# Block 2 of a transformer pair: half of V from unsplit fp32 operands by token halves, and eight modulation steps moved to VectorE

## The chip, the cores and the metric

The kernel runs on one core of a Trainium2 chip. The metric is device microseconds of one execution of the whole program; less is better. Weights are read from HBM once per execution. TensorE (PE) does the matmuls, VectorE (DVE), ScalarE (ACT) and GpSimd (POOL) the rest, and SyncE (SP) issues the weight transfers.

## The reference

The reference runs two blocks on 256 tokens of width 1024, all in fp32. The first is an attention block with layer norm and a mixture of 32 experts, four for each token. The second has two layers (l = 0, 1) whose norms are modulated by a conditioning vector. Cut to what the change touches:

```python
c_act = jax.nn.silu(c)
for i in range(2):
    mod = jnp.einsum('bd,dm->bm', c_act, w_mod[i]) + b_mod[i]
    sh_a, sc_a, gt_a, sh_f, sc_f, gt_f = jnp.split(mod, 6, axis=-1)
    h = modulate(rmsnorm(x, g_mix_pre[i]), sh_a, sc_a)        # h*(1+scale)+shift
    qkv = jnp.einsum('bsd,de->bse', h, w_qkv[i])
    o = attention(q, k, v)                 # stick-breaking for i=0, forgetting for i=1
    x = x + gt_a[:, None, :] * rmsnorm(o @ w_o[i], g_mix_post[i])
    h = modulate(rmsnorm(x, g_ffn_pre[i]), sh_f, sc_f)
    gate = causal_depthwise_conv(h @ w_ffn_gate[i], w_conv[i], b_conv[i])
    y = (jax.nn.silu(gate) * (h @ w_ffn_up[i])) @ w_ffn_down[i]
    x = x + gt_f[:, None, :] * rmsnorm(y, g_ffn_post[i])
```

## The kernel before, in words

Tokens stand in two halves of 128 (t = 0, 1). All weights come through one DMA queue of SP in the order of a list that is written out in `make_stream` and `stream_l2`. Its items are units of 128 x 2048 fp32, 1 MB each. Two units that follow each other share a slot of 2 MB. There are five slots `wu_m`, one `wu_x` and three `wu_y`; the last two kinds are open from the first attention or the first norm until the later experts. A transfer is issued when `take`, which hands units to the program in the order of the list, has moved past both units of an older slot. So what is loaded ahead is limited by slots, and a pair counts as one slot whatever stands in it.

In block 2 nearly every product is made of split operands. `split` turns a unit into a high part wH (a cast on ACT) and a rest wL (a subtraction on DVE), two pieces each; the activations have hH and hL likewise. `mm3` then runs three fp32r matmuls, high by high, low by high and high by low (lines 161 to 163). An FFN unit of gate or up is 48 such matmuls of 256 columns. `pre` makes the normed and modulated h: xs on DVE, transposes on PE, hF from scale and shift (ACT and DVE), then hH and hL. In the gate/up loop of `ffn`, unit n is multiplied while unit n+1 is split; behind that split stands the work on the unit before: for a gate unit the convolution on DVE and silu on ACT, for an up unit the product cv with the gate on DVE, its cast aH on ACT and its rest aL on DVE. Each engine runs its instructions in order.

The modulation vectors, six of 1024 for each layer, come in groups (l, g) of two vectors, and each group takes eight steps, one unit of w_mod each. A step on PE (`mod_step`, line 264) is four fp32 matmuls on strips of 32 columns. On DVE (`mod_dve`, lines 316 and 318) a step is two operations over 1024 columns into `macc`; `mod_sum` then adds the partitions with four matmuls, and `flush_mod` transposes the result into place. Before, groups (0, 1) and (1, 0) are DVE's, in the attention loop and in the down stage of layer 0; the rest are PE's: `fill` puts them where PE has little to do, in numbers set by `MOD_A`, `MOD_PRE` and `MOD_MID`. A group that is interrupted leaves its partial sum in `mpart`, and DVE adds it at the end. `warm` issues bf16 matmuls whose result nobody reads. The MoE ends in `norm2`, the second layer norm; V is the first product of each layer, two units for each half of its columns, followed in layer 1 by the forget gate (`strips`, line 580).

The core of the stream's bookkeeping, in which a freed pair lets the next transfer go:

```python
            if i % 2 == 0:
                self.pools[self.where[i - 2]][1] += 1
                self.pump()
```

Of the kernel before, what the change touches and what calls it, by code (L numbers as in the profile page):

```python
# [18 lines left out]
P = 128  # L19
# [42 lines left out]
class Stream:  # L62


    def __init__(self, nc, srcs):
        self.nc = nc
        self.srcs = srcs
        self.pools = {}
        self.order = []
        self.tiles = {}  # L70
        self.where = {}
        self.issued = 0
        self.taken = 0
# [19 lines left out]
    def pump(self):  # L93
        while self.issued < self.hold:
            for key in self.order:
                if self.pools[key][1] > 0 and self.issued < self.limit.get(key, 1 << 30):
                    break
            else:
                return
            i = self.issued  # L100
            self.pools[key][1] -= 1
            t = self.pools[key][0].tile([P, 2, UNIT], F32, name=f"wu_{key}", tag=f"wu_{key}")
            n = min(2, len(self.srcs) - i)
            if isinstance(self.srcs[i], Pair):
# [8 lines left out]
            self.issued += n  # L113
# [5 lines left out]
    def take(self):  # L119
        i = self.taken  # L120
        if i > 0:
            self.tiles.pop(i - 1)
            if i % 2 == 0:
                self.pools[self.where[i - 2]][1] += 1
                self.pump()
        self.taken += 1
        return self.tiles[i]

# [8 lines left out]
class Kernel:  # L137
# [45 lines left out]
    def run(self):  # L183
        tc, nc, ap = self.tc, self.nc, self.ap
        with ExitStack() as st:
# [16 lines left out]
            self.prs = keep.tile([P, 2], F32, name="prs")  # L202
            self.mhalf = keep.tile([P, 4], F32, name="mhalf")
# [13 lines left out]
    def make_stream(self):  # L217
# [12 lines left out]
        m(MOD_A)  # L230

# [35 lines left out]
    def fill(self, n, pool, pause=False, tag="acc"):  # L267
# [3 lines left out]
        for i in range(n):  # L271
# [11 lines left out]
            if end:  # L283
                sb = pool.tile([P, 512], F32, name="modsb", tag="modsb", bufs=1)

                def late(sb=sb, ps=self.mps, part=self.mpart, l=l, g=g):
                    if part is None:
                        nc.scalar.copy(sb, ps)
                    else:
                        nc.vector.tensor_tensor(sb, ps, part, op=ALU.add)  # L290
                    self.mod_tail = (sb, l, g)

                self.mps = self.mpart = None
# [5 lines left out]
    def pause_mod(self):  # L299
# [4 lines left out]
        if self.mpart is None:  # L304
            part = self.mpart = self.keep.tile([P, 512], F32, name="mpart", tag="mpart")
            return lambda: self.nc.scalar.copy(part, ps)
        part = self.mpart
        return lambda: self.nc.vector.tensor_tensor(part, ps, part, op=ALU.add)
# [11 lines left out]
    def mod_sum(self, acc, l, g, pool, part, tag="acc"):  # L320
# [7 lines left out]
        if part:  # L328
            nc.vector.tensor_tensor(sb, ps, self.mpart, op=ALU.add)
            self.mpart = None  # L330
        else:
            nc.scalar.copy(sb, ps)
# [269 lines left out]
    def norm1(self):  # L602
# [67 lines left out]
        partial = self.fill(MOD_A - 2, a2, True, "sc")  # L670
# [11 lines left out]
        self.warm(WARM[2], "sc", self.cst.bitcast(BF16))  # L682
# [229 lines left out]
    def norm2(self, banks, lnp):  # L912
        nc = self.nc
# [4 lines left out]
        for t in range(2):  # L918
            self.layer_stats(lambda h: banks[t][h], t, mv, rs)
        nm = m1.tile([P, 2], F32, name="nm2")  # L920
        for t in range(2):
            nc.vector.scalar_tensor_tensor(nm[:, t:t + 1], mv[:, t, 0:1], -1.0, rs[:, t:t + 1], op0=ALU.mult, op1=ALU.mult)
            lo, hi = slice(0, 512), slice(512, D)
            nc.scalar.activation(x[:, t, hi], banks[t][1], AF.Identity, bias=nm[:, t:t + 1], scale=rs[:, t:t + 1])
            nc.vector.scalar_tensor_tensor(x[:, t, lo], banks[t][0], mv[:, t, 0:1], lnp[:, 0, lo], op0=ALU.subtract, op1=ALU.mult)
            (nc.vector if t else nc.gpsimd).tensor_tensor(x[:, t, hi], x[:, t, hi], lnp[:, 0, hi], op=ALU.mult)
            (nc.vector if t else nc.gpsimd).tensor_tensor(x[:, t, hi], x[:, t, hi], lnp[:, 1, hi], op=ALU.add)
            nc.vector.scalar_tensor_tensor(x[:, t, lo], x[:, t, lo], rs[:, t:t + 1], lnp[:, 1, lo], op0=ALU.mult, op1=ALU.add)
# [155 lines left out]

    def spread(self, l, m, gname, a, gg=None):
# [17 lines left out]
    def post(self, t, y, gg, a2, tag, last=False):  # L1103
# [5 lines left out]
        for h in range(2):  # L1109
            nc.scalar.activation(self.junk, y[h], AF.Square, scale=1.0 / 32, accum_out=ss[:, h:h + 1])  # L1110
            if t == 1 and not last:
# [4 lines left out]
        if t == 1 and not last:  # L1116
            self.rms(self.prs[:, 0:1], self.xss[:, 0, :])
        for h in range(2):
            nc.vector.scalar_tensor_tensor(self.x[:, t, hs[h]], tmp[h], ss[:, 2:3], self.x[:, t, hs[h]], op0=ALU.mult, op1=ALU.add)
        if last:  # L1120
# [3 lines left out]
    def attention2(self, l, a, a2):  # L1124
# [5 lines left out]
        vps = [self.bank("mm") for _ in range(2)]  # L1130
# [7 lines left out]
        def first():  # L1138
            if l == 0:
                self.w_next = self.split(self.st.take(), 2)  # L1140

        if l == 0:
            self.warm(WARM[1], "tr", self.cst.bitcast(BF16))
        self.pre(l, "g_mix_pre", 0, a, a2, ("oH", "oL"), MOD_PRE[l], first, vps[0], l == 0, WARM2[l])
        cur = self.w_next
        self.token_unit(vps, self.hH, self.hL, cur, 0, (0, 1), NK)
        hH, hL = self.hH, self.hL
        nxt = self.split(self.st.take(), 2)
        for n in range(1, 4):
            cur = nxt  # L1150
            if n == 2:
                vps = [self.bank("sc") for _ in range(2)]
            self.token_unit(vps, hH, hL, cur, 4 * (n % 2), (0, 1), NK)
            nxt = self.split(self.st.take(), 2)
# [125 lines left out]
        for i in range(10):  # L1280
# [20 lines left out]
            if stick and i == 6:  # L1301
                self.mod_sum(macc, 0, 1, a2, DVE_MOD[0, 1] > 0)
# [42 lines left out]
    def ffn(self, l, a, a2):  # L1345
# [26 lines left out]
        cvs = {}  # L1372
        for n in range(NF):
# [12 lines left out]
            cur = self.split(self.st.take(), 2)  # L1386
            if pend is not None:
# [30 lines left out]
        if l == 0:  # L1418
            self.mod_sum(macc, 1, 0, a2, False, "sc")
        for t in range(2):  # L1420
# [86 lines left out]
```

## Time and profile before

| what | value |
|---|---|
| median of 3 runs | 1715.05 us (1714.19 to 1716.04) |
| the profiled execution | 1715.33 us, its span 1713.7 us |
| busy share of the span | PE 97%, DVE 43%, ACT 28%, POOL 5% |
| DMA over the span | 585 MB, 341 GB/s in the mean |
| MoE | from about 115 to 1051 us |
| layer 0 / layer 1 of block 2 | from about 1058 / 1384 us |

The time is measured by the device, the span runs from the first to the last record of the profile, so 1.6 us lie outside it. Shares of busy time are means over the whole span; a stage's limit is read from its own waits. Matmul records of PE overlap, so the time of one is read from start to start; an fp32 matmul leaves two records.

### The profile page before, as it was taken

The page shows a single profiled execution, that of the slowest core. Times are in us where ns is not written, and L with a number is a line of the kernel's source. Part 1 is how long each engine was busy: PE and PEld are TensorE (multiplying, and loading weights), DVE is VectorE, ACT ScalarE, POOL GpSimd, SP SyncE. Part 2 cuts the span into 40 slices and gives each one's busy share as a digit, 9 for nine tenths or more (in the row PEclk, how much of TensorE's full clock was granted, in tenths as well). Part 3 has the DMA queues.
Part 4 walks back from the last instruction along what each step waited for, and adds up shares of the span by engine and source line. Part 5 has one row for each costly group of instructions (what it writes and reads, how often), then busy time and mean ns, then how long its engine had stood idle before and what let it go on. Part 6 is the DMA issues. An engine that isn't in the chain of part 4 may idle for free.

```text
span 1713.7 us, 22958 instructions
## 1 busy us (share of the span) xinstructions
PE 1658.3 (97%) x9678; PEld 980.9 (57%) x9678; DVE 739.9 (43%) x1196; ACT 484.6 (28%) x806; POOL 77.8 (5%) x113
## 2 busy tenths in 40 slices
PE   9999999999999999999899997999999999999998
PEld 7973333333333333333333333886999869889996
DVE  5662121221212212121122115896666866776654
ACT  4530000000001000000010002555555365565543
POOL 0000000000000020000000001121000003100000
PEclk9999999999999999999999999999999999999999
DMA  9879999999999999999999999856855966485430
GB/s 294 323 279 427 428 428 428 428 427 428 426 427 428 428 428 427 427 427 427 426 428 428 428 427 414 345 197 235 328 196 197 373 266 221 161 333 188 181 123 25
DMA packets 59090, 584.85 MB, mean 341 GB/s; under 512 B 8816, under 2 KB 10312, under 8 KB 13544
## 3 DMA queue, kind: packets, MB, share of 16 engines
q1 hardware_dynamic: 57176, 577.95, 82.1%
q0 software_dynamic: 1808, 5.41, 1.3%
q8 instruction: 77, 1.26, 0.3%
q14 instruction: 29, 0.24, 0.0%
HBM read 582.05 MB, written 1.28 MB: 340 GB/s over the span
## 4 chain that ended last, share of the span: by engine, by line
PE 40%; DMA 6%; DVE 3%; issue 1%; ACT 1%; POOL 0%; DVEq 0%; POOLq 0%; ACTq 0%
DMA wu_m<-w_dn 6%; PE ps_mm L161 5%; PE ps_mm L163 5%; PE ps_mm L162 5%; PE ps_sc L161 3%; PE ps_sc L162 3%; PE ps_sc L163 3%; PE ps_mm L738 3%; PE ps_tr L806 2%; PE modps L264 2%; PE ps_acc L161 1%; PE ps_acc L163 1%; PE ps_acc L162 1%; DVE macc L318 1%; DVE wL L156 1%
## 5 line engine op out<-in xcount | busy, mean ns | idle before, releaser
L156 DVE TENSOR_TENSOR wL<-wu_m,wH 128x1024 fp32r<-128x1024 f32 x226 | 266.5, 1222 | 132.9 <-ACT wH L155 128.8
L738 PE MATMUL ps_mm<-wu_m,xg 128*64 128x512 f32 x1200 | 279.1, 600 | 5.5 <-DMA wu_m<-w_gu 5.1
L155 ACT CAST wH<-wu_m 128x1024 fp32r<-128x1024 f32 x226 | 225.8, 1049 | 95.0 <-PE ps_mm L162 66.1
L806 PE MATMUL ps_tr<-wu_m,aT 128*64 128x512 f32 x800 | 179.7, 595 | 19.2 <-DMA wu_m<-w_dn 19.2
L161 PE MATMUL ps_mm<-hH,wH 128*128 128x256 f32 x608 | 174.9, 288 | 0.0
L738 PEld LDWEIGHTS ps_mm<-wu_m,xg 128*64 128x64 f32 x1200 | 79.7, 137 | 165.8 <-issue 143.8
L163 PE MATMUL ps_mm<-hL,wH 128*128 128x256 f32 x608 | 172.0, 283 | 0.2 <-DVE hL L1082 0.2
L162 PE MATMUL ps_mm<-hH,wL 128*128 128x256 f32 x608 | 171.9, 283 | 0.0
L806 PEld LDWEIGHTS ps_tr<-wu_m,aT 128*64 128x64 f32 x800 | 57.0, 137 | 138.2 <-issue 101.2
L161 PEld LDWEIGHTS ps_mm<-hH,wH 128*128 128x128 f32 x608 | 116.4, 191 | 7.8 <-issue 6.5
L163 PEld LDWEIGHTS ps_mm<-hL,wH 128*128 128x128 f32 x608 | 116.5, 192 | 0.4 <-DVE hL L1082 0.4
L162 PEld LDWEIGHTS ps_mm<-hH,wL 128*128 128x128 f32 x608 | 116.5, 192 | 0.0
L810 DVE SCALAR_TENSOR_TENSOR yL<-ps_tr,gs,yH 128x512 fp32r<-128x512 f32 x32 | 24.0, 751 | 204.9 <-ACT yH L809 204.9
L718 ACT COPY gs<-ps_tr 128x512 f32<-128x512 f32 x32 | 18.8, 586 | 330.1 <-PE ps_tr L715 330.1
L792 DVE COPY gs<-ps_tr 128x1 f32<-128x1 f32 x32 | 5.1, 159 | 235.7 <-ACT s L790 235.7
L738 PE MATMUL ps_mm<-wu_y,xg 128*64 128x512 f32 x448 | 103.5, 598 | 1.1 <-DMA wu_y<-w_gu 1.1
L162 PE MATMUL ps_sc<-hH,wL 128*128 128x256 f32 x352 | 99.7, 283 | 0.0
L161 PE MATMUL ps_sc<-hH,wH 128*128 128x256 f32 x352 | 99.6, 283 | 0.0
L163 PE MATMUL ps_sc<-hL,wH 128*128 128x256 f32 x352 | 99.6, 283 | 0.0
L738 PE MATMUL ps_mm<-wu_x,xg 128*64 128x512 f32 x400 | 91.2, 598 | 0.0
L809 ACT ACTIVATE yH<-ps_tr,gs 128x512 fp32r<-128x512 f32 x32 | 22.0, 687 | 233.3 <-PE ps_tr L806 233.3
L753 ACT ACTIVATE sg<-g 128x512 f32<-128x512 f32 x32 | 20.2, 630 | 212.4 <-DVE g L752 212.4
(344 smaller groups left out, 2472.7 us busy)
## 6 DMA issues: line engine op xcount, KB each, us to landing
wu_m<-w_gu SPq DMA_DIRECT2D x75, 2048.0 KB, 25.6
wu_m<-w_dn SPq DMA_DIRECT2D x48, 2048.0 KB, 26.1
wu_y<-w_gu SPq DMA_DIRECT2D x28, 2048.0 KB, 35.7
wu_x<-w_gu SPq DMA_DIRECT2D x25, 2048.0 KB, 24.6
wu_m<-w_mod SPq DMA_DIRECT2D x48, 1024.0 KB, 7.1
wu_m<-w_fg_u SPq DMA_DIRECT2D x44, 1024.0 KB, 8.5
wu_y<-w_dn SPq DMA_DIRECT2D x14, 2048.0 KB, 38.1
wu_m<-w_qk SPq DMA_DIRECT2D x24, 1024.0 KB, 8.8
```

What stands on the lines that cost most here:

```text
L155: nc.scalar.copy(h[:, sl], src[:, sl])
L156: nc.vector.tensor_tensor(lo[:, sl], src[:, sl], h[:, sl].bitcast(F32), op=ALU.subtract)
L161: mm(out, lh, rh, start=start, stop=False)
L162: mm(out, ll, rh, start=False, stop=False)
L163: mm(out, lh, rl, start=False, stop=stop)
L264: self.nc.tensor.matmul(ps[32 * j:32 * j + 32, :], self.cact[:, k:k + 1].to_broadcast([P, 32]), u[:, 512 * j:512 * j + 512], start=start, ...
L718: nc.scalar.copy(gs, g)
L738: mm(ab[i][64 * h:64 * h + 64, :], self.chunk(xg, k), u[:, c:c + 512], start=False, stop=k == NK - 1, tile_position=(0, 64 * h))
L753: nc.scalar.activation(sg, g, AF.Sigmoid, scale=1.702)
L806: nc.tensor.matmul(o[64 * h:64 * h + 64, :], lhs, u[:, c:c + 512], start=f == 0, stop=f == NK - 1, tile_position=(0, 64 * h))
L809: nc.scalar.activation(yH, o, AF.Copy, scale=gate)
L810: nc.vector.scalar_tensor_tensor(yL, o, gate, yH.bitcast(F32), op0=ALU.mult, op1=ALU.subtract)
```

## The change

Three things change, and with them the order of work.

First, `begin` takes the place of `pre` and of the first two V units in both layers. The first half of V is made of 16 fp32 matmuls from hF and the weight units as they are, eight for t = 0 and then eight for t = 1; the two units are not split. hH and hL, which the other products need, are made after them. `norm2` and `post` are ordered so that the norm of t = 0, its xs and its transposes (`turn0`) stand ahead of those of t = 1.

Second, the eight steps of group (1, 1) go from PE to DVE, into the gate/up loop of layer 0 at n = 2, 4, ..., 16. The sum stands at n = 18, the flush at n = 20. With that, the other steps are spread anew: four in norm1 (before three), four in norm2 (before five), eight ahead of FFN 0 (before ten), two at the end of FFN 0 (before six at the start of layer 1), six ahead of FFN 1 (before eight). Instead of an addition on DVE a matmul of the identity with `mpart` puts a partial sum back into PSUM, at the start of norm2's steps and of FFN 1's.

Third, the units ahead of the MoE are 21 and not 20, and a `HOLE` is added so that the experts' pairs stay whole: the last w_mod unit has a slot with an empty half. Warm matmuls change too: four times four in norm2, between the steps, for 16 and seven before; none in norm1, where four stood; eight more ahead of FFN 1.

```diff
-MOD_A = 3
-DVE_MOD = {(0, 1): 0, (1, 0): 0}
-WARM = (8, 16, 4)
+MOD_A = 4
+DVE_MOD = {(0, 1): 0, (1, 0): 0, (1, 1): 0}
+GU_MOD = tuple(range(2, 18, 2))
+WARM = (8, 4)
-WARM2 = ((0, 4, 3, 0), (0, 0, 0, 0))
-WARM3 = ((0, 0, 0, 0), (0, 0, 0, 6))
-MOD_PRE = ((5, 0), (6, 0))
+WARM3 = ((0, 0, 0, 0), (8, 0, 0, 6))
+MOD_PRE = (4, 2)
-MOD_MID = ((8, 2), (8, 0))
+MOD_MID = ((8, 0), (6, 0))
...
         m(MOD_A)
+        if len(u) % 2:
+            u.append(HOLE)
...
+                if self.mpart is not None:
+                    nc.tensor.matmul(self.mps, self.ident, self.mpart, start=True, stop=False)
+                    self.mpart = self.mod_first = None
...
+        stats(0)
+        scale(0)
+        shift(0)
+        for h in range(2):
+            self.stat(0, h)
+        spare = self.bank("mm", "warm")
+        junk = self.cst.bitcast(BF16)
+        for i in range(MOD_PRE[0]):
+            self.warm(WARM[1], spare, junk)
+            late = self.fill(1, m2, False, "tr")
+        stats(1)
+        self.rms(self.prs[:, 0:1], self.xss[:, 0, :])
+        scale(1)
...
+        late()
+        self.turn0(xs, "tr", "sc", lambda: self.flush_mod("sc"))
+        self.scale1(0)
+        shift(1)
...
+    def begin(self, l, a, vps):
...
+        def unit(t, j):
+            if len(w) <= j:
+                w.append(self.st.take(j > 0))
+            for kk in range(4):
+                k = 4 * j + kk
+                nc.tensor.matmul(vps[t], hF[:, k, t * P:(t + 1) * P], w[j][:, kk * 512:kk * 512 + 512], start=k == 0, stop=k == NK - 1)
+
+        for k in range(NK):
+            scaled(0, self.tps0, k)
+        unit(0, 0)
+        unit(0, 1)
+        for h in range(2):
+            self.stat(1, h)
+        self.rms(self.prs[:, 1:2], self.xss[:, 1, :])
+        nc.vector.tensor_scalar(xs, self.x[:, 1, :], self.prs[:, 1:2], None, op0=ALU.mult)
+        tps = self.turn_rows(xs, "tr", "acc")
+        for k in range(4):
+            scaled(1, tps, k, True)
+            scaled(1, tps, k + 4)
+        unit(1, 0)
+        unit(1, 1)
...
             cur = self.split(self.st.take(), 2)
+            if l == 0 and n in GU_MOD:
+                self.mod_dve(macc, GU_MOD.index(n), n == GU_MOD[0])
+            if l == 0 and n == GU_MOD[-1] + 2:
+                self.mod_sum(macc, 1, 1, a2)
+            if l == 0 and n == GU_MOD[-1] + 4:
+                self.flush_mod()
             if pend is not None:
                 pend()
...
+            if l == 0 and t == 1:
+                late = self.fill(MOD_PRE[1], a2, True)
+                xs = a.tile([P, D], F32, name="xs0", tag="hL")
+                self.scale1(1)
+                self.turn0(xs, "tr", "tr")
+            self.post(t, (y[t, 0], y[t, 1]), self.gg, a2, "cv", last=l == 1, early=l == 0)
```

In PE's program at the end of the MoE and the start of layer 0, before, ps_tr and ps_sc are banks of transposes, modps is the sum of the modulation, and wH, hH, hL, wL are the split operands of V:

```order
L177 MATMUL warm<-cst 128x512
...
L264 MATMUL modps<-wu_m,cact 32x512 x20
L1061 MATMUL ps_tr<-cst,xs 128x128 x8
L344 MATMUL ps_acc<-cst,modsb 128x128 x4
...
L1061 MATMUL ps_sc<-cst,xs 128x128 x8
...
L161 MATMUL ps_mm<-wH,hH 128x512
L162 MATMUL ps_mm<-wH,hL 128x512
L163 MATMUL ps_mm<-wL,hH 128x512
```

And the same place in PE's program of the change:

```order
L188 MATMUL warm<-cst 128x512
...
L293 MATMUL modps<-mpart,cst 128x512
L278 MATMUL modps<-wu_m,cact 32x512 x4
...
L351 MATMUL ps_sc<-cst,modsb 128x128 x4
L965 MATMUL ps_tr<-cst,xs_5740 128x128 x4
L965 MATMUL ps_sc<-cst,xs_5740 128x128 x4
L1147 MATMUL ps_mm<-wu_m,hF 128x512 x8
L965 MATMUL ps_tr<-cst,xs 128x128 x4
L965 MATMUL ps_acc<-cst,xs 128x128 x4
L1147 MATMUL ps_mm<-wu_m,hF 128x512 x8
L172 MATMUL ps_sc<-wH,hH 128x512
```

The flush now stands ahead of the transposes of token half 0, those of half 1 behind the first eight fp32 matmuls, and the split matmuls begin with the second half of V (ps_sc).

In DVE's program at the start of the gate/up loop of layer 0, before (lines 1361, 1367 and 1369 are convolution, product and rest):

```order
L156 TENSOR_TENSOR wL<-wu_m,wH 128x1024 x4
L1361 SCALAR_TENSOR_TENSOR cv<-ps_mm,cols,cv 128x255 x2
L1361 SCALAR_TENSOR_TENSOR cv<-ps_mm,cols,cv 128x254 x2
L156 TENSOR_TENSOR wL<-wu_m,wH 128x1024 x2
L1367 TENSOR_TENSOR cv<-cv,ps_sc 128x512
L1369 TENSOR_TENSOR aL<-cv,aH 128x512
```

And of the change, where the convolution is line 1442, the product 1448, the rest 1450, and the steps are lines 327 and 329:

```order
L167 TENSOR_TENSOR wL<-wu_m,wH 128x1024 x4
L1442 SCALAR_TENSOR_TENSOR cv<-ps_mm,cols,cv 128x255 x2
L1442 SCALAR_TENSOR_TENSOR cv<-ps_mm,cols,cv 128x254 x2
L167 TENSOR_TENSOR wL<-wu_m,wH 128x1024 x2
L327 TENSOR_SCALAR macc_7076<-wu_m,cact 128x1024 x2
L1448 TENSOR_TENSOR cv<-cv,ps_sc 128x512
L1450 TENSOR_TENSOR aL<-cv,aH 128x512
...
L329 SCALAR_TENSOR_TENSOR macc_7076<-wu_m,cact,macc_7076 128x1024 x2
L1448 TENSOR_TENSOR cv<-cv,ps_sc 128x512
```

A modulation step stands between the wL of an odd unit and the product of the pair before it, once in every two units.

In SP's queue ahead of the MoE, before:

```order
L91 DMA wu_m<-w_out 128x2048 x4
L91 DMA wu_m<-w_mod 128x2048 x3
L105 DMA wu_m<-w_gu 128x4096
L105 DMA wu_x<-w_gu 128x4096
L105 DMA wu_m<-w_gu 128x4096 x2
L105 DMA wu_y<-w_gu 128x4096 x3
```

And of the change:

```order
L92 DMA wu_m<-w_out 128x2048 x4
L92 DMA wu_m<-w_mod 128x2048 x4
L108 DMA wu_x<-w_gu 128x4096
L108 DMA wu_m<-w_gu 128x4096 x2
L108 DMA wu_y<-w_gu 128x4096 x3
```

The fourth w_mod unit has the place of the first pair of w_gu, and one pair of w_gu fewer stands ahead of the wu_y pairs.

## Rows read from the trace of the kernel before

**Rows 1.** The page: busy time by engine; GB/s in 40 slices of the span.
```profile
PE 1658.3 (97%) x9678; PEld 980.9 (57%) x9678; DVE 739.9 (43%) x1196; ACT 484.6 (28%) x806; POOL 77.8 (5%) x113
...
GB/s 294 323 279 427 428 428 428 428 427 428 426 427 428 428 428 427 427 427 427 426 428 428 428 427 414 345 197 235 328 196 197 373 266 221 161 333 188 181 123 25
```

**Rows 2.** Waits of PE, 500 to 1000 us: total, times, longest.
```profile
PE ps_tr L806 <- DMA wu_m<-w_dn: 13.9, 14, 1.3
```

**Rows 3.** Waits of PE, 1051 to 1710 us.
```profile
PE modps L264 <- DVE x L925: 2.7, 1, 2.7
```

**Rows 4.** Timeline of SP's DMA queue: start, us, queue, line, transfer.
```profile
72.63 0.33 SPq L105 DMA_DIRECT2D wu_m<-w_gu  x1
...
112.95 3.83 SPq L105 DMA_DIRECT2D wu_y<-w_gu  x3
```

**Rows 5.** Windows of the early stages (busy by engine, clock, DMA share, GB/s).
```profile
80.00:90.00 10.00, 10.00 (x83) 9.90 (x82) 6.82 (x18) 4.83 (x12) 0.00 (x0) 1.00 0.00 0
...
110.00:115.00 5.00, 5.00 (x23) 4.08 (x22) 3.73 (x7) 0.00 (x0) 0.55 (x1) 1.00 0.29 56
```

**Rows 6.** Timeline, start of layer 0: start, us, engine, line, operation.
```profile
1051.35 1.30 DVE L697 BATCH_NORM_STATS2 bs<-ps_sc 128x6 f32<-128x512 f32 x2 [0.59 <-PE ps_sc L818]
...
1051.72 3.63 PE L177 MATMUL warm<-cst 128*128 128x512 bf16 x16
...
1057.29 0.74 DVE L925 SCALAR_TENSOR_TENSOR x<-ps_acc,mv,lnp 128x512 f32<-128x512 f32 x1
...
1058.08 5.89 PE L264 MATMUL modps<-wu_m,cact 128*32 128x512 f32 x40 [2.74 <-DVE x L925]
...
1063.91 1.09 PE L1061 MATMUL ps_tr<-cst,xs 128*128 128x128 f32 x8
```

**Rows 7.** Timeline of PE, first half of V in layer 0.
```profile
1074.07 0.39 PE L162 MATMUL ps_mm<-wH,hL 128*128 128x512 f32 x1
...
1079.51 0.39 PE L162 MATMUL ps_mm<-wH,hL 128*128 128x512 f32 x1
...
1080.64 0.39 PE L161 MATMUL ps_sc<-wH,hH 128*128 128x512 f32 x1
```

**Rows 8.** Timeline, start of FFN in layer 1.
```profile
1509.31 7.07 PE L264 MATMUL modps<-wu_m,cact 128*32 128x512 f32 x64
...
1516.45 0.59 ACT L288 COPY modsb<-modps 128x512 f32<-128x512 f32 x1 [2.73 <-PE modps L264]
...
1517.24 0.60 PE L344 MATMUL ps_acc<-cst,modsb 128*128 128x128 f32 x4
```

**Rows 9.** Timeline, start of layer 1.
```profile
1383.96 5.36 PE L264 MATMUL modps<-wu_m,cact 128*32 128x512 f32 x48
...
1392.33 0.51 PE L161 MATMUL ps_mm<-wH,hH 128*128 128x512 f32 x1 [1.11 <-ACT hH L1079]
...
1404.12 1.07 PE L580 MATMUL ps_acc<-hF,wf 128*32 128x256 f32 x16
```

**Rows 10.** Timeline of PE in the MoE, line 859.
```profile
682.99 1.12 PE L859 MATMUL ps_sc<-h,cst 128*128 128x512 f32 x2
```

**Rows 11.** Windows: one pair of gate/up units in layer 0.
```profile
1218.18:1229.70 11.52, 11.52 (x98) 11.52 (x97) 7.58 (x10) 6.18 (x9) 0.00 (x0) 1.00 0.80 316
```

**Rows 12.** Timeline of DVE, down stage of layer 0.
```profile
1327.19 1.41 DVE L316 TENSOR_SCALAR macc<-wu_m,cact 128x1024 f32<-128x1024 f32 x2
...
1331.12 2.48 DVE L318 SCALAR_TENSOR_TENSOR macc<-wu_m,cact,macc 128x1024 f32<-128x1024 f32 x2
```

**Rows 13.** Groups of ACT by line, eight pairs of units (1218 to 1310 us).
```profile
L155 ACT CAST wH<-wu_m 128x1024 fp32r<-128x1024 f32 x32 | 31.9, 1045 | 8.8 <-PE ps_mm L163 8.6
```

**Rows 14.** Timeline, gate/up of layer 0.
```profile
1212.98 1.05 ACT L155 CAST wH<-wu_m 128x1024 fp32r<-128x1024 f32 x1 [0.20 <-PE ps_mm L163]
...
1219.83 2.36 DVE L156 TENSOR_TENSOR wL<-wu_m,wH 128x1024 fp32r<-128x1024 f32 x2 [1.83 <-ACT wH L155]
...
1224.30 0.28 PE L161 MATMUL ps_sc<-hH,wH 128*128 128x256 f32 x1
```

More of the change, by code (lines that the diff above doesn't have):

```diff
@@ L117, in resume, with take @@
         self.pump()
-    def take(self):
+    def take(self, hold=False):
         i = self.taken
[L121 to L126, printed above, removed]
+        if self.srcs[i] is HOLE:
+            i += 1
+        if not hold:
+            while self.freed < i:
+                self.tiles.pop(self.freed, None)
+                self.freed += 1
+                if self.freed % 2 == 0:
+                    self.pools[self.where[self.freed - 2]][1] += 1
+                    self.pump()
+        self.taken = i + 1
         return self.tiles[i]
+HOLE = "hole"
 class Pair:
@@ L284, in fill, with late @@
                 sb = pool.tile([P, 512], F32, name="modsb", tag="modsb", bufs=1)
[L286 to L290, printed above, removed]
+                def late(sb=sb, ps=self.mps, l=l, g=g):
+                    nc.scalar.copy(sb, ps)
                     self.mod_tail = (sb, l, g)
-                self.mps = self.mpart = None
+                self.mps = None
                 if i < n - 1:
@@ L303, in pause_mod @@
         ps, self.mps = self.mps, None
[L304 to L308, printed above, removed]
+        part = self.mpart = self.keep.tile([P, 512], F32, name="mpart", tag="mpart")
+        return lambda: self.nc.scalar.copy(part, ps)
     def mod_dve(self, acc, k, first):
@@ L327, in mod_sum @@
         sb = pool.tile([P, 512], F32, name="modsb", tag="modsb", bufs=1)
[L328 to L332, printed above, removed]
+        nc.scalar.copy(sb, ps)
         self.mod_tail = (sb, l, g)
@@ L917, in norm2 @@
         rs = m1.tile([P, 2], F32, name="rs2")
[L918 to L928, printed above, removed]
+        hs = [slice(h * 512, h * 512 + 512) for h in range(2)]
@@ L1110, in post @@
             nc.scalar.activation(self.junk, y[h], AF.Square, scale=1.0 / 32, accum_out=ss[:, h:h + 1])
-            if t == 1 and not last:
+            if t == 1 and not last and not early:
                 self.stat(0, h)
@@ L1115, in post @@
         nc.vector.tensor_tensor(tmp[1], y[1], gg[:, hs[1]], op=ALU.mult)
-        if t == 1 and not last:
+        if t == 1 and not last and not early:
             self.rms(self.prs[:, 0:1], self.xss[:, 0, :])
@@ L1119, in post @@
             nc.vector.scalar_tensor_tensor(self.x[:, t, hs[h]], tmp[h], ss[:, 2:3], self.x[:, t, hs[h]], op0=ALU.mult, op1=ALU.add)
+        if t == 0 and early:
+            for h in range(2):
+                self.stat(0, h)
+            self.rms(self.prs[:, 0:1], self.xss[:, 0, :])
         if last:
@@ L1136, in dve_step @@
             self.mod_dve(macc, k, k == DVE_MOD[0, 1])
[L1138 to L1146, printed above, removed]
+        self.begin(l, a, vps)
         hH, hL = self.hH, self.hL
@@ L1151, in attention2 @@
             if n == 2:
[L1152 to L1154 removed]
+                vps = [self.bank(tags[1]) for _ in range(2)]
+            if n > 1:
+                self.token_unit(vps, hH, hL, cur, 4 * (n % 2), (0, 1), NK)
+                nxt = self.split(self.st.take(), 2)
             if stick and n < 3 and len(dve) > 6:
@@ L1423, in ffn @@
                 self.flush_mod("sc")
-            if t == 1 and l == 0:
-                self.w_next = self.split(self.st.take(), 2)
             down(last, nxt, (t,))
-            self.post(t, (y[t, 0], y[t, 1]), self.gg, a2, "cv", last=l == 1)
+            if l == 0 and t == 1:
[4 more added lines that the diff above has]
+            self.post(t, (y[t, 0], y[t, 1]), self.gg, a2, "cv", last=l == 1, early=l == 0)
+        if l == 0:
+            late()
 def pack(inputs):
```

66 lines of the change are left out of this document (53 added, 13 removed).

## The prediction

> **What bounds the kernel now.** I read the page first, then the PE waits by stretch, then SP's timeline of transfers, then the PE, ACT and DVE timelines at four places. On the page PE is busy 97% of the span and DMA moves 426 to 428 GB/s in every slice from the fourth to the 24th [rows 1], which is the stretch from about 130 to 1030 us, the MoE. These two lines leave open which of the two bounds that stretch. The waits settle it: between 500 and 1000 us PE waited 13.9 us for w_dn in the m slots alone, in 14 waits [rows 2]. So the MoE ends when its last weights have landed. Early in it PE lives off what was loaded ahead; that lead is used up by the middle, and from there each megabyte that comes later moves the end of the MoE. In block 2 no listed wait is for DMA; the longest is 2.7 us for an x of norm2 [rows 3]. There PE's own instructions and the short chains between stages set the time.
>
> The profiled execution took 1715.33 us with a span of 1713.7, 0.28 above the median of 1715.05. I add to 1715.33 and take 0.28 off at the end. A measurement of this kernel tells 0.2%, 3.4 us, from no change.
>
> **The early transfers.** Before, SP issues three w_mod units, then at 72.63 us a pair of w_gu into the slot just freed. From 80 to 90 us nothing moves, from 110 to 115 only 56 GB/s [rows 5]; saturation starts with the three wu_y pairs at 112.95 [rows 4]. After, the units ahead of the MoE are 21 and a HOLE, 11 pairs and not 10, so the slot of 72.63 takes a w_mod unit and an empty half, and the w_gu pair moves behind. 2 MB of expert weights that were loaded in free time must now pass while DMA is full: 2.097 MB by 0.428 MB/us = 4.9 us. Since the queue is full from 113 us to the end of the MoE, the last w_dn lands that much later: **+4.9**. Bounds: 0, if PE's pace and not DMA's were what ends the MoE; 2.45, if only the megabyte of w_mod counted and the hole cost nothing. I take the upper end, because the waits for w_dn run through the second half of the MoE. One w_mod unit more is multiplied in norm1 (0.86 us) where four warm matmuls go (0.9): nothing.
>
> **The start of layer 0.** Let T0 be the first statistics of norm2 (1051.35). Before, PE ran 16 warm matmuls, sat 2.74 us for x, ran 40 modulation matmuls (5 steps), transposes and the split of h; the second half of V began at 1080.64 [rows 6, 7], T0 + 29.3. Per matmul, the split product takes (1079.51 − 1074.07)/24 = 0.227 us [rows 7]. One modulation step, two fp32 passes of 512 columns on each of four strips that run side by side, takes the difference of 8 and 6 steps, (7.07 − 5.36)/2 = 0.855 us [rows 8, 9]; that is my price for one full-width fp32 matmul of 512 columns. The first half of V was 48 × 0.227 = 10.9 us and becomes 16 × 0.855 = 13.7: **on PE alone the change costs 2.8 us per layer**. The trace has a worse bound too: the one full-width fp32 matmul of line 859, two records, took 1.12 us [rows 10], 0.26 more each, 4.2 us per layer.
>
> The Trainium skill speaks against this part: FP8 and Floating Point Precision, section TensorE Precision Notes, says that true FP32 makes four passes through the PE array. Four passes of 0.227 against three would make the half of V 14.5 us and my forecast 0.8 longer per layer; the 0.855 of the step is a little below four passes, and I go by the row.
>
> What the change saves is the chain. After, PE needs from T0 + 0.4: 16 warm 3.6, the restoring matmul 0.86, four steps 3.4, so it is at T0 + 8.3; copy of the modulation 0.6 and flush 0.6 [rows 8], transposes of token half 0 1.1 [rows 6], first hF 0.3 behind the last of them, eight fp32 matmuls 6.84, transposes of half 1 1.1 and first hF 0.15, eight more 6.84: T0 + 25.8. DVE's and ACT's part for half 0 (statistics, two scales, two shifts, square sums, about 8.9 us at 0.74 an operation [rows 6]) ends just ahead of it, and half 1 has the first eight matmuls as cover; if that cover fell short, each microsecond of it would be PE's. hH, hL and the split of the third unit fit behind them. **−3.5**, between −2.5 (PE goes on waiting about a microsecond) and −4.
>
> **FFN of layer 0.** Two modulation steps leave its start, where hH and hL are the later ones: **−0.25**. In its gate/up loop eight steps are added on DVE, one in each pair of units from the second, and behind them a sum of four matmuls (0.85) and a flush (0.6): **+1.4** on PE.
>
> The steps themselves look free: DVE is busy 7.58 of the 11.52 us of a pair of units [rows 11], and a step is two operations, 2.40 us once the 0.08 by which records overlap are off [rows 12]. But in order, ACT and DVE form a closed chain: cast, wL, product with cv, aH, cast, wL, convolution, silu, and then the next cast. Around it there is one wait for PE, ahead of one of the two casts: 8.6 us in eight pairs [rows 13], 1.07 a pair. The rest of the 11.52, 10.45, is the chain's own, and the step stands in it, between wL and the product for which aH waits: 12.85. So each pair runs 1.33 us later than PE's pace. In the first pair with a step the wait for PE is only 0.20 [rows 14]; the first step costs 1.4, being another operation, priced by the same operation in the down stage [rows 12]: 1.4 + 7 × 2.4 − 0.2 − 7 × 1.07 = 10.5 us late at the last. The first half of a wL is ready at 1219.83 + 1.18 = 1221.0, and PE takes it up at 1224.30 [rows 14]: 3.3 us ahead. PE stands for the remainder: **+7.2**, range 5 to 9, and 0 if the step finds room that the order doesn't show. Queued behind the step on DVE are the product and aL, then the next wL, for which PE waits.
>
> **The start of layer 1.** T1 is the end of FFN 0's down product (1383.96). Before, the forget strips, which follow the first half of V, began at 1404.12 [rows 9], T1 + 20.2. After: two steps 1.71, transposes 1.1, first hF 0.6, 6.84, transposes 1.1, 0.15, 6.84: T1 + 18.3. The wait of 1.11 for hH [rows 9] goes, as do four steps. The chain of half 1 (update of x, sums, scaling) is by my count some 7 us long from T1 and has the 10.2 us until its transposes as cover; past that, PE would wait. **−1.9**; 1.0 to 2.4. A flush of 0.55 leaves the attention loop: **−0.55**.
>
> **FFN of layer 1.** Eight steps (6.8 us) become restoring matmul, six steps and eight warm ones: 0.86 + 5.1 + 1.7: **+0.85**.
>
> **Sum.** 4.9 − 3.5 − 0.25 + 1.4 + 7.2 − 1.9 − 0.55 + 0.85 = +8.15; 1715.33 + 8.15 − 0.28 = **1723.2**.
>
> **Rivals.**
> The loop keeps up (no stall in gate/up): DVE has 3.9 us free per pair and needs 2.4. It speaks against it that the room lies ahead of the casts and behind silu. The price is 7.2: 1716.0, no change. It decides when the chain's own time per pair with a step stays at or below 11.52, that is, if 1.3 us of what I count as chain is overlap. Chance 0.24.
> The lead is made up (MoE ends as before), but the loop stalls: 1718.3, at the edge between no change and slower. For it: PE has buffers of 18 MB to live off early on. Against it: DMA is never below 426 GB/s, so there is no room in which to catch up. Chance 0.12.
> Both hold: 1711.1, faster. Chance 0.17; a kernel whose waits all go leaves only PE's work, about +1.5, and the chains' −6.
> The fp32 half of V takes 1.1 us per matmul, as the nearest full-width row: 8.4 us on top of the forecast, 1731.6. The 128 weight columns would have to be loaded in the open. Chance 0.05.
> The forecast itself: 0.42.
>
> **Numbers.** Faster: 0.17 and, with the chains at their better ends, 0.08 of the first rival: 0.25. Same: 0.16 of the first and 0.06 of the second: 0.22. Slower: the forecast, the rest of the second and the fp32 rival: 0.53. Range: from 1711.0, which keeps most of the case in which both hold, to 1726.5, the forecast with loop and chains at their worse ends; left out are about half of the fp32 rival's and the lower part of the faster case.
>
> **What the profile after would show.** The lead: the scatter of the last expert ends near 1056 and not 1051, w_dn waits start earlier. The loop: in FFN 0 gate/up PE waits for wL, about 1.3 us per pair from the fourth or fifth step, ACT no longer waits for PE. Layer 0: V's second half at T0 + 25.8, fp32 matmuls 0.43 us apart per record. Layer 1: forget strips at T1 + 18.3. The prediction is wrong if gate/up runs at 11.52 us per pair throughout, or if the MoE ends within a microsecond of 1051.

## The result and the profile after

The changed kernel took 1725.68 us (median of 4 runs, 1724.16 to 1726.58) against 1714.65 for the kernel before: ratio 1.0062, 95% interval 1.0045 to 1.008. It is slower by 0.62%, which is more than the 0.2% that a measurement tells from no change. The profiled execution took 1724.92 us with a span of 1722.4, against 1715.33 and 1713.7. So the traces differ by 8.7 us of span and the medians by 11.0; the readings below explain the 8.7. The other 2.3 lie in the executions that were profiled: before, it is 0.7 above its median, after, 0.8 below, and 0.9 us more of it lies outside the span.

The page of the changed kernel, busy time by engine and GB/s in 40 slices:

```profile
PE 1658.3 (96%) x9589; PEld 970.0 (56%) x9591; DVE 743.8 (43%) x1194; ACT 475.9 (28%) x806; POOL 78.1 (5%) x111
...
GB/s 290 300 278 429 427 428 428 427 427 428 427 428 427 428 427 426 428 427 427 427 427 428 427 427 419 332 196 273 298 253 228 372 214 193 145 286 208 185 109 25
```

PE is busy for 1658.3 us in both kernels [rows 1]. So by these records all of the 8.7 us is time in which PE stood still, and a share of busy time says nothing of where. The stages do. Each number here is the difference between the starts of two PE instructions (the first row: the first statistics of norm2 on DVE), the same two in both kernels:

| stage | before, us | after, us | difference | forecast |
|---|---|---|---|---|
| up to the first statistics of norm2 (T0) | 1051.35 | 1056.45 | +5.1 | +4.9 |
| T0 to the second half of V, layer 0 | 29.29 | 26.16 | −3.1 | −3.5 |
| from there to the steps ahead of FFN 0 | 103.31 | 103.81 | +0.5 | 0 |
| from there to the second unit of gate/up | 17.04 | 16.90 | −0.1 | −0.25 |
| from there to the down product | 121.33 | 128.24 | +6.9 | +8.6 |
| the down product to its last unit | 56.11 | 56.14 | 0.0 | 0 |
| from there to the forget strips, layer 1 | 25.69 | 23.73 | −2.0 | −1.9 |
| from there to the start of FFN 1 | 105.19 | 105.70 | +0.5 | −0.55 |
| from there to its second unit | 16.89 | 17.80 | +0.9 | +0.85 |
| the rest | 175.48 | 175.48 | 0.0 | 0 |

SP's timeline of early transfers in the changed kernel answers to [rows 4]:

```profile
50.65 20.74 SPq L92 DMA_DIRECT2D wu_m<-w_mod  x4
88.11 0.33 SPq L108 DMA_DIRECT2D wu_x<-w_gu  x1
...
113.46 1.28 SPq L108 DMA_DIRECT2D wu_y<-w_gu  x3
```

No pair of w_gu goes out near 72 us any more; the fourth w_mod unit has its slot, and the next pair follows at 88.

The start of layer 0 in the changed kernel, timeline (start, us, engine, line, operation), answers to [rows 6, 7]:

```profile
1056.45 1.30 DVE L704 BATCH_NORM_STATS2 bs<-ps_sc 128x6 f32<-128x512 f32 x2 [0.59 <-PE ps_sc L825]
...
1062.57 1.06 PE L278 MATMUL modps<-wu_m,cact 128*32 128x512 f32 x8
...
1063.57 1.04 PE L188 MATMUL warm<-cst 128*128 128x512 bf16 x4
...
1064.53 1.06 PE L278 MATMUL modps<-wu_m,cact 128*32 128x512 f32 x8
...
1066.30 0.65 PE L351 MATMUL ps_sc<-cst,modsb 128*128 128x128 f32 x4 [0.71 <-ACT modsb L304]
...
1067.96 7.13 PE L1147 MATMUL ps_mm<-wu_m,hF 128*128 128x512 f32 x16
...
1074.93 0.60 PE L965 MATMUL ps_tr<-cst,xs 128*128 128x128 f32 x4
...
1076.04 7.13 PE L1147 MATMUL ps_mm<-wu_m,hF 128*128 128x512 f32 x16
...
1082.61 0.79 PE L172 MATMUL ps_sc<-wH,hH 128*128 128x512 f32 x1
1083.24 0.40 PE L173 MATMUL ps_sc<-wH,hL 128*128 128x512 f32 x1
```

The waits of PE of 2.74 us for x [rows 3] and, at 1067.90, of 1.20 for hH are gone. With the first of them went a stretch at the lower clock. Two windows of the kernel before and one of the changed kernel (the seventh number is the granted clock as a share of 2.4 GHz):

```profile
1058.00:1061.00 3.00, 2.92 (x16) 0.80 (x20) 2.48 (x5) 1.78 (x6) 0.92 (x2) 0.51 1.01 421
1061.00:1064.00 3.00, 3.00 (x29) 0.70 (x22) 1.67 (x3) 2.97 (x6) 0.88 (x2) 1.00 0.89 322
...
1061.00:1064.00 3.00, 3.00 (x22) 0.68 (x15) 2.93 (x8) 0.69 (x2) 1.06 (x2) 1.00 1.00 418
```

Before, PE stood from 1055.35 to 1058.08, and the steps behind that ran near the lower level of 1.2 GHz until 1061. The five of them took 5.83 us (1058.08 to 1063.91 [rows 6]) where 5 × 0.855 are 4.28, so about 1.55 us of the old start was clock. In the changed kernel the granted clock of this start is 1.00 throughout.

A round of four warm matmuls and a step takes 1.96 us (1064.53 − 1062.57), and eight fp32 matmuls with what follows them stand open in PE's row: 6.97 us from 1067.96 to the transposes at 1074.93.

The gate/up loop of layer 0 in the changed kernel, timelines of DVE and ACT, answers to [rows 13, 14]:

```profile
1260.86 2.36 DVE L167 TENSOR_TENSOR wL<-wu_m,wH 128x1024 fp32r<-128x1024 f32 x2 [1.69 <-ACT wH L166]
1263.13 2.47 DVE L329 SCALAR_TENSOR_TENSOR macc<-wu_m,cact,macc 128x1024 f32<-128x1024 f32 x2
1265.53 0.68 DVE L1448 TENSOR_TENSOR cv<-cv,ps_sc 128x512 f32<-128x512 f32 x1
...
1266.24 0.62 ACT L1449 CAST aH<-cv 128x512 fp32r<-128x512 f32 x1 [4.47 <-DVE cv L1448]
1266.77 1.99 ACT L166 CAST wH<-wu_m 128x1024 fp32r<-128x1024 f32 x2
```

The waits of PE between 1205 and 1320 us (total, times, longest):

```profile
PE ps_mm L173 <- DVE wL L167: 4.1, 5, 0.8
```

And PE's timeline at the first matmuls of two gate units, one pair apart:

```profile
1255.41 0.28 PE L172 MATMUL ps_mm<-hH,wH 128*128 128x256 f32 x1
...
1268.02 0.28 PE L172 MATMUL ps_mm<-hH,wH 128*128 128x256 f32 x1
```

The product waits behind the step, aH waits for the product (4.47 us idle on ACT), and the cast behind aH starts at once: ACT no longer waits for PE there. A pair takes 12.61 us and not 11.52. Before, PE had no wait in this stretch.

The start of layer 1, PE's timeline, answers to [rows 9]:

```profile
1393.23 1.92 PE L278 MATMUL modps<-wu_m,cact 128*32 128x512 f32 x16
1395.08 1.09 PE L965 MATMUL ps_tr<-cst,xs 128*128 128x128 f32 x8
1396.29 7.13 PE L1147 MATMUL ps_sc<-wu_m,hF 128*128 128x512 f32 x16
...
1404.37 7.13 PE L1147 MATMUL ps_sc<-wu_m,hF 128*128 128x512 f32 x16
```

Steps, transposes of one half and its V stand without a gap.

### The profile page after: what moved, and what is told of

The parts are those of the page before. It is cut to its first block, busy times and chain, and to the rows that moved or that the text cites. A ratio compares the mean times of both kernels' runs of the same rounds, so it can differ in the third digit from the quotient of the medians.

```text
span 1722.4 us, 22764 instructions
## 1 busy us (share of the span) xinstructions
PE 1658.3 (96%) x9589; PEld 970.0 (56%) x9591; DVE 743.8 (43%) x1194; ACT 475.9 (28%) x806; POOL 78.1 (5%) x111
## 4 chain that ended last, share of the span: by engine, by line
PE 32%; DVE 8%; DMA 7%; ACT 3%; issue 2%; POOL 0%; DVEq 0%; POOLq 0%; ACTq 0%
DMA wu_m<-w_dn 6%; PE ps_mm L172 4%; PE ps_mm L174 3%; PE ps_mm L173 3%; DVE wL L167 3%; PE ps_mm L745 3%; PE ps_tr L813 2%; PE ps_sc L172 2%; PE ps_sc L173 2%; PE ps_sc L174 2%; DVE macc L329 2%; PE ps_acc L172 1%; PE ps_acc L174 1%; PE ps_acc L173 1%; ACT wH L166 1%
## 5 line engine op out<-in xcount | busy, mean ns | idle before, releaser
L167 DVE TENSOR_TENSOR wL<-wu_m,wH 128x1024 fp32r<-128x1024 f32 x218 | 257.5, 1222 | 118.3 <-ACT wH L166 117.7
L745 PE MATMUL ps_mm<-wu_m,xg 128*64 128x512 f32 x1296 | 297.6, 599 | 5.3 <-DMA wu_m<-w_gu 5.3
L166 ACT CAST wH<-wu_m 128x1024 fp32r<-128x1024 f32 x218 | 217.7, 1048 | 82.3 <-PE ps_mm L173 63.1
L745 PEld LDWEIGHTS ps_mm<-wu_m,xg 128*64 128x64 f32 x1296 | 86.3, 137 | 177.3 <-issue 155.5
L813 PE MATMUL ps_tr<-wu_m,aT 128*64 128x512 f32 x704 | 158.9, 595 | 15.2 <-DMA wu_m<-w_dn 14.4
L813 PEld LDWEIGHTS ps_tr<-wu_m,aT 128*64 128x64 f32 x704 | 50.2, 137 | 119.5 <-issue 89.4
L745 PE MATMUL ps_mm<-wu_y,xg 128*64 128x512 f32 x464 | 107.2, 598 | 2.1 <-DMA wu_y<-w_gu 2.1
L772 DVE COPY aT<-ps_tr 128x512 f32<-128x512 f32 x32 | 22.1, 691 | 127.0 <-PE ps_tr L770 127.0
```

Source lines behind the costliest of these rows:

```text
L166: nc.scalar.copy(h[:, sl], src[:, sl])
L167: nc.vector.tensor_tensor(lo[:, sl], src[:, sl], h[:, sl].bitcast(F32), op=ALU.subtract)
L745: mm(ab[i][64 * h:64 * h + 64, :], self.chunk(xg, k), u[:, c:c + 512], start=False, stop=k == NK - 1, tile_position=(0, 64 * h))
L772: nc.vector.tensor_copy(aT, tp)
L813: nc.tensor.matmul(o[64 * h:64 * h + 64, :], lhs, u[:, c:c + 512], start=f == 0, stop=f == NK - 1, tile_position=(0, 64 * h))
```

## The experiments

The theory: two things cost most of the time, each by a mechanism of its own. The late end of the MoE comes from 2 MB of expert weights that are no longer loaded ahead, and the stall in gate/up from a closed chain of ACT and DVE in which the step stands. The rivals: the MoE ends later because of the work in norm1 or by chance, and gate/up stalls from the mere load (DVE's work, the bytes of w_mod). The comparisons below are with the changed kernel's 1725.68 and, for the ratios, with the kernel before, which ran beside each group (1714.67, 1714.37 and 1714.48).

**The feed restored.** Three w_mod units ahead of the MoE, no hole, five steps in norm2.

```diff
-MOD_A = 4
-WARM = (8, 4)
-MOD_PRE = (4, 2)
+MOD_A = 3
+WARM = (8, 3)
+MOD_PRE = (5, 2)
...
-        self.fill(1, a2, False, "sc")
+        partial = self.fill(1, a2, True, "sc")
...
-        partial = self.fill(MOD_A - 3, a2, True, "sc")
```

> The changed kernel with three w_mod units ahead of the MoE instead of four and no hole, five steps in norm2 instead of four, three warm matmuls ahead of each instead of four. If the lost 2 MB of expert weights cause the later end of the MoE, the first statistics of norm2 come back from 1056.4 to about 1051.4 (5 us earlier), the start of layer 0 is about 0.6 longer for the fifth step, and the whole is 4 to 4.5 us shorter than the changed kernel's 1725.7, near 1721. If the later end comes from something else (the steps of the MoE itself, chance of the run), the MoE still ends near 1056 and the time is at or above 1725.7.

Measured: 1718.42 us, ratio to before 1.0022 (1.0013 to 1.0032). T0 is 1051.32, 5.1 earlier than in the changed kernel; the start of layer 0 is 0.9 longer (27.05). That is the 4.2 of the theory; the time fell by 7.3, more than the 4 to 4.5 expected. Another 1.8 us came from where I had expected nothing: layer 1's attention took 103.93 and not 105.70 (see the exchange of cm and ggd below). These two make up the 6.0 by which the spans of the two profiled executions differ. The remaining difference of the medians, 1.3, has no row.

**An idle pair in the kernel before.** The opposite test: nothing but a slot of 2 MB more ahead of the MoE, whose two units nobody uses.

```diff
         m(MOD_A)
+        u.extend(self.mod_unit(0, 0, k) for k in range(2))
...
         partial = self.fill(MOD_A - 2, a2, True, "sc")
+        self.st.take()
+        self.st.take()
```

> The kernel before with two more w_mod units in one slot ahead of the MoE, which are loaded and not used; nothing else changes, on no engine. If the slot alone makes the loss, the MoE ends 4.9 us later than 1051.35 and the whole takes about 1720. If the later end in the changed kernel came from the work in norm1, this kernel takes 1715, as before.

Measured: 1719.58 us, ratio 1.0027 (1.0017 to 1.0038), 4.9 us above the kernel before. Its first statistics of norm2, on DVE:

```profile
1055.27 1.30 DVE L700 BATCH_NORM_STATS2 bs<-ps_sc 128x6 f32<-128x512 f32 x2 [0.59 <-PE ps_sc L821]
```

T0 is 3.9 us later than before and every stage behind it is as before within 0.1 us. So a slot that is taken away from the experts costs 3.9 us by T0 and 4.9 by the medians, against 4.9 worked out, with no change of any engine's work.

**The steps behind the convolution.** The same steps in odd units, behind `pend()`.

```diff
-GU_MOD = tuple(range(2, 18, 2))
+GU_MOD = tuple(range(3, 18, 2))
...
-            if l == 0 and n in GU_MOD:
-                self.mod_dve(macc, GU_MOD.index(n), n == GU_MOD[0])
...
             if pend is not None:
                 pend()
+            if l == 0 and n in GU_MOD:
+                self.mod_dve(macc, GU_MOD.index(n), n == GU_MOD[0])
```

> The changed kernel with the eight VectorE steps in odd units of gate/up (n = 3, 5, ..., 17), behind the convolution and not ahead of the product; the amount of work and the bytes are the same. If the closed chain of cast, wL, product, aH, cast, wL, convolution, silu causes the stall, a step that stands beside silu and the next cast (1.74 us of the 2.40 covered) leaves the chain at 10.45 + 0.66 = 11.1 us per pair, under PE's 11.52: the five waits of about 1.1 us disappear and the time falls by 5 to 6 us to about 1720. If the load of the engines or the reads of w_mod stall PE, the pairs stay at 12.6 us and the time stays at 1725.7.

Measured: 1720.37 us, ratio 1.0034 (1.0021 to 1.0046), 5.3 below the changed kernel. Its gate/up loop, timelines of DVE and ACT:

```profile
1264.70 1.65 DVE L1442 SCALAR_TENSOR_TENSOR cv<-ps_mm,cols,cv 128x255 f32<-128x255 f32 x4
1266.26 2.47 DVE L329 SCALAR_TENSOR_TENSOR macc<-wu_m,cact,macc 128x1024 f32<-128x1024 f32 x2
1268.65 2.36 DVE L167 TENSOR_TENSOR wL<-wu_m,wH 128x1024 fp32r<-128x1024 f32 x2
...
1266.44 0.63 ACT L1444 ACTIVATE cv<-cv 128x512 f32<-128x512 f32 x1 [2.18 <-DVE cv L1442]
1267.10 2.00 ACT L166 CAST wH<-wu_m 128x1024 fp32r<-128x1024 f32 x2
...
1272.86 1.05 ACT L166 CAST wH<-wu_m 128x1024 fp32r<-128x1024 f32 x1 [0.60 <-PE ps_mm L174]
```

While DVE does the step, ACT does silu and the next cast. ACT waits for PE again (0.60 us), and PE has no wait between 1205 and 1320 us. The same work and bytes at another place in the order take 123.01 us for the stage and not 128.24. So load is not the cause. The down stage became 1.1 us longer (57.19): the flush now stands in the last pair ahead of it.

**Both.**

> Both edits: three w_mod units ahead of the MoE and the steps behind the convolution. If the two losses are independent, the savings add: 1725.7 - 4.3 - 5.7 = about 1715.7, no change against before. If the steps' stall and the feed share a cause, or the stall was only hidden by the late feed, less than the sum is saved, about 1720.

Measured: 1714.21 us, ratio 1.0000 (0.9991 to 1.001): no change against before. The stages show 27.04 for the start of layer 0, 123.02 for gate/up and 103.94 for layer 1's attention: the savings of the stages add, and the shorter attention comes with the feed, as it did alone. (The medians fell by 11.5, the two single savings are 7.3 and 5.3.)

**No warm matmuls ahead of FFN 1** (on top of both).

```diff
-WARM3 = ((0, 0, 0, 0), (8, 0, 0, 6))
+WARM3 = ((0, 0, 0, 0), (0, 0, 0, 6))
```

> The kernel of the run with both repairs, without the eight warm matmuls ahead of FFN 1. If they stand openly on PE's path, the start of FFN 1 (from the restoring matmul to the second unit) is 1.6 to 1.9 us shorter and the time near 1712.5. If they hide another wait (the flush, or the lower clock without them), less than 0.5 us is saved.

Measured: 1712.56 us, ratio 0.9991 (0.9982 to 1.0). The stage falls from 17.80 to 16.12: the eight stood openly on PE's path.

**One warm matmul per step in norm2** (on top of both).

```diff
-WARM = (8, 3)
+WARM = (8, 1)
```

> The kernel with both repairs and one warm matmul ahead of each step of norm2 instead of three. If PE's own instructions bound the start of layer 0, ten matmuls of 0.227 us less bring the second half of V from 27.0 to about 24.9 us after the first statistics, and the time to about 1712. If DVE's and ACT's chain of token half 0 bounds it (its xs ends 8.1 us after the first statistics), or PE's clock falls, less is saved or something is lost.

Measured: 1712.36 us, ratio 0.9989 (0.9979 to 0.9998). The second half of V comes at T0 + 24.90 and not 27.04. The granted clock in windows of this start, this kernel:

```profile
1051.00:1057.00 6.00, 6.00 (x40) 1.38 (x40) 5.79 (x12) 1.45 (x4) 0.57 (x1) 1.00 1.01 419
1057.00:1063.00 6.00, 5.16 (x33) 2.41 (x26) 3.81 (x9) 2.77 (x8) 1.06 (x2) 1.00 1.02 425
```

The seventh number is the clock, 1.00 of 2.4 GHz in both. So PE's own instructions bound this start, and PE went on at full clock without the ten.

**The steps at the start of layer 1 moved ahead of FFN 1** (on top of the run without warm matmuls).

```diff
-MOD_PRE = (5, 2)
-MOD_MID = ((8, 0), (6, 0))
+MOD_PRE = (5, 0)
+MOD_MID = ((8, 0), (8, 0))
```

> As the run without warm matmuls ahead of FFN 1, and the two steps that stood at the start of layer 1 stand ahead of FFN 1 instead (eight there, none before, no partial sum and no restoring matmul). If the two steps stand openly on PE's path because xs of token half 0 is ready 0.2 us after them, layer 1's fp32 matmuls begin 1.4 to 1.7 us earlier, and the start of FFN 1 is at most 0.9 longer: 0.6 to 1.7 less than the run without warm matmuls. If half 1's chain is what V waits for, the gain at the start is given back by a wait of the second eight matmuls.

Measured: 1712.41 us, ratio 0.9989 (0.998 to 0.9999). Layer 1's start fell from 23.73 to 22.15, FFN 1's grew from 16.12 to 16.90: 0.8 us by the stages. The two medians differ by 0.15 us, so the gain can be read in the stages and not in the time; this profiled execution reached T0 0.6 later.

**All together.**

> All of these together: three w_mod units ahead of the MoE, steps behind the convolution, one warm matmul per step in norm2, none of the eight ahead of FFN 1, no steps at the start of layer 1. If the stages are independent the savings add to 1709 to 1711, 0.2 to 0.3% below the kernel before; if PE's clock falls with fewer warm matmuls, it is at 1714 or above.

Measured: 1710.83 us, ratio 0.998 (0.9971 to 0.9989): faster than the kernel before. Layer 1's attention took 104.68 here, 0.6 to 0.8 more than in the other runs with the feed restored; no run explains that.

**cm ahead of ggd.** In the changed kernel, layer 1's attention had grown by 0.5 where I had counted a flush less. In its last pairs of heads that kernel's POOL timeline shows:

```profile
1483.77 0.53 POOL L1181 DMA_DIRECT2D ggd<-ggr  x1 [10.55 <-DVE ggr L1179]
1485.60 0.57 POOL L1182 DMA_DIRECT2D gg<-ggd  x1 [1.31 <-DMA ggd<-ggr]
1486.18 0.78 POOL L1282 TENSOR_SCALAR_AFFINE_SELECT cm<-cm 128x256 f32<-128x256 f32 x2
...
1487.63 0.73 POOL L1276 DMA_DIRECT2D cm<-cumd  x1
...
1496.82 0.41 POOL L1282 TENSOR_SCALAR_AFFINE_SELECT cm<-cm 128x256 f32<-128x256 f32 x1 [1.85 <-DMA cm<-cumd]
```

POOL's queue stands 10.55 us for DVE, then issues the last load of the decay sums cm, which is masked only at 1496.82. PE's waits from 1425 us to the end of the stage, for p, nl and pT, are 0.7, 0.4 and 0.3 us. The exchange, on the changed kernel itself:

```diff
-            if i == 8 - 2 * l:
+            if stick and i == 8:
                 rows()
...
                     if i < 7:
                         load_cum(i + 1)
+                    if i == 6:
+                        rows()
```

> The changed kernel with one exchange in layer 1's attention: POOL's last load of the decay sums (cm) is issued ahead of the two transfers that spread the post norm's gain (ggd, gg), which stand ahead of it before and hold POOL's queue until DVE has made their source. If that queue makes the attention of layer 1 take 105.7 us instead of the 104.6 that I had counted, it falls to 104 to 104.6 us and the whole by 1 to 1.7 us, to about 1724.3. If the last cm lands late because of the weight transfers beside it, the attention stays at 105.4 to 105.7.

Measured: 1722.6 us, ratio 1.0046 (1.0031 to 1.0062), 3.1 below the changed kernel. The attention is at 104.10, and from 1425 us on PE has no wait in it. POOL's timeline:

```profile
1480.82 0.72 POOL L1275 DMA_DIRECT2D cm<-cumd  x1 [0.45 <-DVE st L1322]
1481.54 0.72 POOL L1276 DMA_DIRECT2D cm<-cumd  x1
1484.45 0.53 POOL L1181 DMA_DIRECT2D ggd<-ggr  x1 [2.19 <-DVE ggr L1179]
```

So the exchange is worth 1.6 us of the stage. The rest of the gain is more than the stages show (the spans differ by 1.1), and it stays open.

The order of POOL's queue is not the whole cause, because it is the same in the kernel before and in the run with the feed restored. The second transfer of the last cm is issued 76.2 us behind the forget strips in the changed kernel, 76.0 with the feed restored and 77.5 before. What differs is how long it takes from there to its masking: 9.2, 5.1 and 4.5 us. SP's and POOL's timelines with the feed restored, and SP's of the changed kernel:

```profile
1483.22 0.74 POOL L1275 DMA_DIRECT2D cm<-cumd  x1
1488.29 1.13 POOL L1281 TENSOR_SCALAR_AFFINE_SELECT cm<-cm 128x256 f32<-128x256 f32 x1 [1.08 <-DMA cm<-cumd]
1490.52 0.33 SPq L92 DMA_DIRECT2D wu_m<-w_mod  x1
...
1486.19 0.81 SPq L92 DMA_DIRECT2D wu_m<-w_mod  x2
```

In the changed kernel SP issues two units of w_mod 0.7 us ahead of cm; with the feed restored the pair ahead goes out at 1473.39 and the next one only after the masking. The run with the steps behind the convolution, which has the changed kernel's feed, has the same neighbours (SP at 1482.38, cm at 1483.09) and needs 8.7 us. With the exchange cm is issued 5 us ahead of that pair. So the changed feed seems to have moved a pair of weights onto cm, which was late in the queue already; no run moves that pair alone, so this half of the cause is argued.

**All, with cm first and the steps one pair earlier.**

```diff
-GU_MOD = tuple(range(3, 18, 2))
+GU_MOD = tuple(range(1, 16, 2))
```

> The run with all repairs, with the exchange of cm and ggd, and with the VectorE steps one pair earlier in gate/up (n = 1, 3, ..., 15, sum at 17, flush at 19), so that the flush no longer stands in the last pair ahead of the down product. If the down stage's extra 1.05 us came from that flush, it is 56.1 us again, the attention of layer 1 is near 104, and the time is about 1 to 1.7 us below the run with all repairs, near 1709.3. If the first step at n = 1 meets silu's table load and PE waits for it, gate/up gets longer by what the down stage gains.

Measured: 1708.41 us, ratio 0.9966 (0.9952 to 0.9979): faster than the kernel before by 0.34%, and than the changed kernel by 1%. The down stage is back at 56.14, layer 1's attention at 104.05, gate/up at 123.08. Its PE waits in block 2, the longest:

```profile
PE ps_mm L172 <- ACT hH L1117: 1.1, 1, 1.1
PE ps_sc L351 <- ACT modsb L304: 0.7, 1, 0.7
```

## Why the prediction was right

The time lay in the range, the sign was as forecast, and the size was +8.15 forecast, +8.7 in the profiled spans and +11.0 in the medians. That the sum came so close is in part luck: gate/up was put 1.7 too high, layer 1's attention 1.05 too low and the first three stages together 1.1 too low. Point by point:

- **The feed**, +4.9: T0 came 5.1 later. Shown from both sides: the slot given back brings T0 back by 5.1, the slot taken from the kernel before costs 3.9 by T0 and 4.9 in the median. T0 lies between 1056.4 and 1057.0 in the three kernels with the half-empty slot, and between 1050.7 and 1052.2 in the eight with neither that nor the idle pair. The bound of 2.45, by which only the megabyte counts, falls.
- **The start of layer 0**, −3.5: measured −3.1. The fp32 matmuls cost what the modulation step had told (6.97 us for eight with their tail, 6.84 forecast), not the 1.12 each of line 859 [rows 10]. What I had too low is the stretch ahead of them: warm matmuls and steps in turn take 1.96 us a round where 4 × 0.227 + 0.855 = 1.76, so PE is behind its count by 0.8 after four rounds. The second half of V then starts with a slow first matmul (1082.61 to 1083.24), part of the +0.5 of the stage behind it, which I had put at nothing. Of what went, I had named the wait for x; the 1.55 us of lower clock behind it stood in the 29.3 that I took from the row, so the forecast holds it without knowing it.
- **Gate/up**, stall +7.2: the largest miss. The stage grew by 6.9, of which the sum and the flush, by their own rows and forecast, are 1.4, so the stall is about 5.5. (The last run keeps both without the stall: its stage is 1.7 longer than before and 5.2 shorter than the changed kernel's, so the stall is 5.2 by that.) The mechanism is as forecast: pairs of 12.61 us against my 12.85, with PE waiting for wL. The chain per pair was counted 0.24 too long; over the seven pairs between the first and the last step that is 1.7, all or nearly all of the miss.
- **The start of layer 1**, −1.9: measured −2.0. **FFN 1**, +0.85: +0.9. **FFN 0**, −0.25: −0.1.
- **The flush that leaves layer 1's attention**, −0.55: measured +0.5. The step that failed is that I counted the flush alone and not the small transfers of that stage. The last load of cm stands behind ggd and gg on POOL, and in the changed kernel it landed so late that PE waited. With cm ahead, the stage is at 104.1, 1.1 below the kernel before; if the flush is worth its 0.55, cm's lateness cost the kernel before about as much, and its trace has one wait of PE for p of 0.6 us.

The first rival (the loop keeps up) is what the placement behind the convolution does; ahead of the product it didn't. The second rival (the lead is made up) is refuted by the idle pair. The fp32 rival is refuted by the row of line 1147.

Which part of the change is worth having is plain only in part. The two starts of layers, with V by token halves and fewer modulation steps ahead of it, are 5.1 us shorter together; how much of that is the fp32 matmuls' and how much the steps' was not separated. The four steps that left the start of layer 1 are 3.4 us by their price of 0.855, more than the 2.0 gained there, and the eight steps that left PE altogether are 6.8, more than the 6.1 us by which the last run beats the kernel before. So no run shows that the fp32 half of V is worth having by itself. The other two parts gave away more than the starts gained, through a slot and a place in DVE's order, and only 1.4 to 1.7 us through work that they add.

## What to carry to other kernels

Where a step is put onto an engine that has room, look for a closed chain through that engine: a chain's slack is the one wait in its circle (here 1.07 us in 11.52), not the engine's idle time (3.9). Count prefetch in slots: in a stage that DMA bounds, a half-empty slot taken in the free time ahead of it costs the whole pair (5.1 us of T0 for 2 MB here). A wait at the head of a queue that issues small transfers (here 10.55 us on POOL) delays the ones behind it, and whether that costs anything depends on how late they land. And look at the granted clock behind a long wait of PE: here 2.74 us of waiting cost 1.55 more.

## What the runs showed of the hardware

- Eight fp32 matmuls of 512 columns on the full width took 6.97 us from the first to what follows, 0.87 each, 3.8 times the 0.227 of one fp32r pass [rows 7]. The Trainium skill, FP8 and Floating Point Precision, section TensorE Precision Notes, gives four passes for true FP32; the 3.8 of the trace is close to that.
- A change between bf16 warm matmuls and fp32 modulation steps cost about 0.2 us a round over the two prices alone: 1.96 against 1.76 with four warm matmuls, 1.32 against 1.08 with one (1052.62 to 1053.94 in that run).
- The last cm took 9.2 us from its issue to its masking in the changed kernel and 5 us with the feed restored (issued at 1483.22, masked at 1488.29). In the first a pair of weight transfers was issued 0.7 us ahead of it, in the second none in the 8 us before; no run moves that pair alone.
- In the kernel before, PE stood for 2.74 us ahead of the steps of norm2; the granted clock was 0.51 from 1058 to 1061 us, next to the lower level of 1.2 GHz, and 1.00 from 1061 on. With one warm matmul per step and no such wait it was 1.00 in every window read from 1051 to 1069.
